# A hybrid mLSTM and delta-rule block on one core: a fourth buffer for weights, more products from rounded halves, gate rows through DRAM, and an earlier split of the delta rule's output

## The chip, the cores and the metric

One core of one Trainium2 chip runs one layer of a bidirectional encoder block. The metric is the device time of one launch in microseconds (us). A profile of one further execution gives the engines' work: PE (TensorE, matrix products), DVE (VectorE), ACT (ScalarE), POOL (GpSimd, here used nearly only to issue DMAs) and SP (SyncE, only issues DMAs).

## The reference, cut to what matters

256 tokens, 2048 channels, all of it in float32:

```python
mod = silu(c) @ ada_w + ada_b                     # six rows of 2048: shift, scale, gate, twice
h = rms_norm(x, norm_mix_w) * (1 + scale_m) + shift_m
proj = h @ w_in                                   # split into a_q a_k a_v a_o, b_qkv, b_z, gates, merge
# branch A: mLSTM, 4 heads, dk 256, dv 512, forwards and backwards
y_a = (sigmoid(a_o) * rms_norm(h_a)) @ w_branch_a
# branch B: gated delta rule, 16 heads, dk = dv = 128, forwards and backwards
qkv = silu(centred_depthwise_conv(b_qkv, gdn_conv_w))
y_b = (rms_norm(o_b) * silu(b_z)) @ w_branch_b
x = x + gate_m * ((g_a * y_a + g_b * y_b) @ w_out)          # gate_m is row 2 of mod
hf = rms_norm(x, norm_ffn_w) * (1 + scale_f) + shift_f
x = x + gate_f * ((silu(gt) * up) @ w_down)                 # gate_f is row 5 of mod
return rms_norm(x, norm_final_w)
```

Both branches are needed in scores: the delta rule needs k·k and q·k of each head, the mLSTM needs q·k and then the sum of the decayed scores times v.

## The kernel before, in words

**Products.** Large products are made from *rounded halves*: of a float32 array `w`, ACT writes `wh`, rounded to the type float32r, and DVE writes `wl = w - wh` (the helper `split`, or the same two instructions inside a job). A product is then `xh·wh + xl·wh + xh·wl`, three passes on PE. A few products still take float32 operands as they are; PE runs such a product as two instructions. Among them are the delta rule's scores `ks` (L571, two of 128x512 a head), the mLSTM's sums over v `ph` (L977, six of 128x512 a head) and the gate rows (`row`, L1088, four of 128x512 for each of two rows).

**Jobs.** Weights stream in as 1 MB tiles `raw` from a pool with three buffers, by DMAs that SP issues in a fixed order. The same three buffers also take the rows of `ada_w` for the sums that make `mod` ("background": `ada_part` loads one 1 MB tile, and one DVE instruction, L126, reduces it). `fjob` multiplies one 128-column block (tiles `raw_b`, `raw_a`), `tjob` one group of 512 columns: four tiles `u`, each in two halves `wh_x_u_0` and `wh_x_u_2`, twelve products of 128x512 for each half. A tile is free for SP when DVE has read it for the last time, and SP's list stands in line: a load whose buffer isn't free holds up all loads behind it.

**Order of the work.** A stage 0 makes `mod`'s first rows, `x` and the first heads (until about 131 us). Then the delta rule runs for four groups of four heads: `gdn_phase1` for each head (convolution, decay, scores `ks`), `gdn_invert` and `gdn_blocks` for a group, and `gdn_phase2` for each pair of heads (a chain of small products `p`, `pa`, `pb`, `pc`, `po`, `px` with ACT and DVE steps between them). Independent jobs (`b`, `a`, `z`, `v`, `o`, `ma`, `mb`) are put between these steps as *fillers*. At the end of a pair the outputs go through DRAM: ACT writes `obt`, stores it (`ob_d`), and POOL loads a group of four heads as `o` (L866). `o_split` makes `obh` and `obl` of it for the projection `yb`. After the delta rule's buffers are given up, `mlstm(h)` for heads 0 and 1, later 2 and 3, is placed between `yb`'s halves. It loads `mkq`, `vt`, `sgo` and twice `bc` on POOL (L917 to L924), makes decays by scans on DVE (`mdec`, L928 to L931), scores `psc` (PE), multiplies both (L946 to L949), and makes `pden` and `ph`. Then come `ya`, `o` with the first residual, gate/up (`gt`, `up`) and down (`d`) of the feed-forward part.

**What sets the order.** The kernel is written as one sequence of instructions; a scheduler of the framework then makes a list for each engine, which runs in that order. Instructions that are wrapped in `order(...)` keep the order in which they are written among themselves, whatever their engine; the rest are placed where the scheduler sees them ready. So an edit in one place can move instructions in others. PSUM is split into four banks for jobs and four for the rest.

Of the kernel before, what the change touches and what calls it, by code (L numbers as in the profile page):

```python
# [52 lines left out]
def hybrid_block(ctx: ExitStack, tc: tile.TileContext, xr, nfr, crow, pk_d, cst_d, ada2, ada4, win0, winb, wint, wba, wbb, wo, wgu, wd, out, dbg=None):  # L53
# [6 lines left out]
    cp = pool(ctx, "cp")  # L60
    st = pool(ctx, "st")
# [35 lines left out]
    c1 = st.tile([1, D], F32, tag="raw", bufs=3, name="c1")  # L97
# [20 lines left out]
    ada_in = [st, "raw", 3]  # L118
# [11 lines left out]


# [16 lines left out]
    def fjob(name, src, done):  # L148

        ps = acc_ps.tile([P, 512], F32, tag="acc", name=f"acc_{name}")  # L150
        o = ps[:, :T]
        raw = st.tile([P, KB, P], F32, tag="raw", bufs=3, name=f"raw_{name}")
        nc.sync.dma_start(raw, src)
        for k0 in range(0, KB, 8):
            wh = st.tile([P, 8, P], F32R, tag="wh", bufs=3, name=f"wh_{name}_{k0}")
            wl = st.tile([P, 8, P], F32R, tag="wl", bufs=3, name=f"wl_{name}_{k0}")
            S.activation(wh, raw[:, k0 : k0 + 8], AF.Copy)  # L157
            V.tensor_tensor(wl, raw[:, k0 : k0 + 8], wh.bitcast(F32), ALU.subtract)  # L158
            for k in range(8):
                for i, x in enumerate((hh, hl)):  # L160
                    PE.matmul(o, wh[:, k], both(x, k0 + k).rearrange("p a b -> p b a"), start=k0 + k + i == 0, stop=False)  # L161
# [7 lines left out]
    def tjob(name, chunks, xh, xl, done, early=0, by_token=None, steps=1):  # L169
# [6 lines left out]
        def halves(u, k0):  # L176
            if u not in raws:
                raws[u] = st.tile([P, 4, 512], F32, tag="raw", bufs=3, name=f"raw_{name}_{u}")
# [3 lines left out]
            order(S.activation(wh, raws[u][:, k0 : k0 + 2], AF.Copy), early)  # L182
            order(V.tensor_tensor(wl, raws[u][:, k0 : k0 + 2], wh.bitcast(F32), ALU.subtract), early)  # L183
            return wh, wl
# [261 lines left out]
    with ExitStack() as s0:  # L446
# [18 lines left out]
        def loads(b):  # L465
            ra = [w0.tile([P, D + 2], F32, tag="ra", bufs=5, name=f"ra{b}_{i}") for i in range(2)]
            raw = st.tile([P, N0, P], F32, tag="raw", bufs=3, name=f"raw0_{b}")
# [73 lines left out]
    def gdn_phase1(h):  # L541
# [13 lines left out]
        sq = fr.tile([P, T], F32, tag="sqq", bufs=1, name=f"sqq{h}")  # L555
# [11 lines left out]
        mi = fr.tile([P, 4, P], F32, tag="mi", bufs=1, name=f"mi{h}")  # L567
        kss = []
        for t in range(2):
            ks = gps(f"ks{h}_{t}")  # L570
            PE.matmul(ks, kq[:, 0, t * P : (t + 1) * P], kq, start=True, stop=True)  # L571
# [343 lines left out]
    def mlstm(h):  # L915
# [19 lines left out]
        for t in range(2):  # L935
# [17 lines left out]
            (0, 0): [(dec[:, 0, 0:P], 0)],  # L953
            (0, 1): [(dec[:, 0, P:256], 0), (dec[:, 0, 256:384], 1)],
            (1, 0): [(dec[:, 1, 256:384], 0), (dec[:, 1, 0:P], 1)],
            (1, 1): [(dec[:, 1, P:256], 1)],
        }
        pd_ = gps(f"pden{h}")
        for (d, t), terms in src.items():
            for i, (w, s) in enumerate(terms):  # L960
                PE.matmul(pd_[:, 2 * t + d : 2 * t + d + 1], w, ones1, start=i == 0, stop=i == len(terms) - 1)
# [8 lines left out]
        yield  # L970
        for t in range(2):
            pn = []
            for d in range(2):
                ph = gps(f"ph{h}_{t}_{d}")
                terms = src[d, t]
                for i, (w, s) in enumerate(terms):
                    PE.matmul(ph, w, vt[:, s], start=i == 0, stop=i == len(terms) - 1)  # L977
# [4 lines left out]
            yield  # L982
# [19 lines left out]
    def y_b(g):  # L1002
# [6 lines left out]
        return tjob(f"yb{g}", [wbb[g, u] for u in range(4)], obh, obl, done)  # L1009
# [30 lines left out]
    for g in range(3):  # L1040
        fill(2)
        o_split(g, o4s[g])
# [10 lines left out]
    mg = mgp.tile([P, 2, D], F32, name="mg")  # L1053

# [8 lines left out]
    for g in range(4):  # L1063
        if g == 3:
            every[0] = 0
        run(y_a(g, mgh, mgl))
    while len(background) > 2:
        sums()
# [11 lines left out]
    def row(part, dst, rp, factor=1.0):  # L1080

        for g in range(4):
            dg = rp.tile([P, 4, P], F32, tag="dg", bufs=2, name=f"dg{part}_{g}")
            for e in range(4):
                c = part * KB + 4 * g + e
                V.tensor_scalar(dg[:, e], ident, mod[:, c : c + 1], factor, ALU.mult, ALU.mult)
            pr = gps(f"row{part}_{g}")
            PE.matmul(pr, ones, dg.rearrange("p e c -> p (e c)"), start=True, stop=True)  # L1088
            S.activation(dst[:, g * 512 : (g + 1) * 512], pr, AF.Copy)

    gm = wp.tile([P, D], F32, name="gm")
    row(2, gm, wp, 0.5)
# [64 lines left out]
    ada_in[:] = [st, "raw", 3]  # L1157
# [84 lines left out]
    row(5, gf, dp)  # L1242
# [134 lines left out]
```

## Time and profile before

| | us |
|---|---|
| median of three runs (1995.4, 1998.9, 2001.5) | 1998.9 |
| the profiled execution, its time | 1998.51 |
| its span from the first to the last instruction | 1996.5 |
| PE busy | 1935.0 (97%) |
| DVE busy | 1392.7 (70%) |
| ACT busy | 1020.6 (51%) |
| POOL busy | 94.7 (5%) |
| DMA: moved in all | 485.64 MB, mean 243 GB/s |

PE's busy time counts from the start of a product to its modelled end, and successive products overlap, so a busy PE still says nothing of how densely it works; the starts of successive products do. An engine's idle time matters here where PE has nothing to do.

### The profile page before, as it was taken

The page shows a single profiled execution, that of the slowest core. Times are in us where ns is not written, and L with a number is a line of the kernel's source. Part 1 is how long each engine was busy: PE and PEld are TensorE (multiplying, and loading weights), DVE is VectorE, ACT ScalarE, POOL GpSimd, SP SyncE. Part 2 cuts the span into 40 slices and gives each one's busy share as a digit, 9 for nine tenths or more (in the row PEclk, how much of TensorE's full clock was granted, in tenths as well). Part 3 has the DMA queues.
Part 4 walks back from the last instruction along what each step waited for, and adds up shares of the span by engine and source line. Part 5 has one row for each costly group of instructions (what it writes and reads, how often), then busy time and mean ns, then how long its engine had stood idle before and what let it go on. Part 6 is the DMA issues. An engine that isn't in the chain of part 4 may idle for free.

```text
span 1996.5 us, 26938 instructions
## 1 busy us (share of the span) xinstructions
PE 1935.0 (97%) x10310; PEld 1697.5 (85%) x10310; DVE 1392.7 (70%) x2099; ACT 1020.6 (51%) x1558; POOL 94.7 (5%) x181
## 2 busy tenths in 40 slices
PE   8998999999999889999899999899999999999997
PEld 6887889988989888989777888688888888888886
DVE  5777987778988787865677779765666665555554
ACT  3145757754774566555453444554444444444443
POOL 0001200110100010100100000000000000000000
PEclk9998999999999999999999999999999999999999
DMA  9986674567676665876787679457676675555553
GB/s 400 420 355 193 197 231 169 177 200 256 209 237 222 212 197 208 284 284 238 298 313 259 241 279 413 166 218 261 235 267 237 232 268 199 208 205 198 209 200 138
DMA packets 78322, 485.64 MB, mean 243 GB/s; under 512 B 10201, under 2 KB 15585, under 8 KB 23793
## 3 DMA queue, kind: packets, MB, share of 16 engines
q1 hardware_dynamic: 63360, 450.95, 62.2%
q0 software_dynamic: 7520, 17.88, 4.3%
q10 hardware_dynamic: 7314, 15.10, 2.0%
q8 instruction: 81, 1.33, 0.3%
q14 instruction: 47, 0.39, 0.1%
HBM read 467.07 MB, written 16.82 MB: 242 GB/s over the span
## 4 chain that ended last, share of the span: by engine, by line
PE 78%; DMA 9%; DVE 7%; ACT 4%; issue 2%; ACTq 0%; POOL 0%; SPq 0%; DVEq 0%; POOLq 0%
PE acc_up L200 4%; PE acc_up L203 4%; PE acc_up L201 4%; PE acc_d L203 4%; PE acc_d L201 4%; PE acc_d L200 4%; PE acc_gt L201 4%; PE acc_gt L200 4%; PE acc_gt L203 4%; DMA ra<-ada 3%; PE acc_b L161 3%; PE acc_o L203 2%; PE acc_o L200 2%; PE acc_o L201 2%; PE acc_a L161 2%; DMA raw_b<-winb 2%
## 5 line engine op out<-in xcount | busy, mean ns | idle before, releaser
L183 DVE TENSOR_TENSOR wl_d<-raw_d,wh_d 128x1024 fp32r<-128x1024 f32 x88 | 107.7, 1224 | 102.3 <-ACT wh_d L182 100.3
L183 DVE TENSOR_TENSOR wl_up<-raw_up,wh_up 128x1024 fp32r<-128x1024 f32 x88 | 107.7, 1225 | 101.2 <-ACT wh_up L182 101.2
L126 DVE SCALAR_TENSOR_TENSOR ada<-ada,crow 128x2048 f32<-128x2048 f32 x64 | 146.4, 2288 | 41.9 <-DMA ada<-ada 41.8
L182 ACT ACTIVATE wh_d<-raw_d 128x1024 fp32r<-128x1024 f32 x88 | 93.0, 1057 | 128.5 <-PE acc_d L201 122.8
L182 ACT ACTIVATE wh_gt<-raw_gt 128x1024 fp32r<-128x1024 f32 x88 | 92.9, 1056 | 120.7 <-PE acc_gt L201 73.2
L182 ACT ACTIVATE wh_up<-raw_up 128x1024 fp32r<-128x1024 f32 x88 | 93.0, 1057 | 120.5 <-PE acc_up L201 72.9
L183 DVE TENSOR_TENSOR wl_gt<-raw_gt,wh_gt 128x1024 fp32r<-128x1024 f32 x88 | 107.1, 1223 | 68.1 <-ACT wh_gt L182 47.3
L161 PE MATMUL acc_b<-hh,wh_b 128*128 128x256 f32 x576 | 140.8, 285 | 7.7 <-ACT wh_b L157 7.7
L161 PE MATMUL acc_b<-hl,wh_b 128*128 128x256 f32 x576 | 141.2, 286 | 0.0
L200 PE MATMUL acc_gt<-wh_gt,hfh 128*128 128x512 f32 x352 | 135.7, 385 | 0.1
L201 PE MATMUL acc_gt<-wh_gt,hfl 128*128 128x512 f32 x352 | 135.0, 384 | 0.0
L200 PE MATMUL acc_up<-wh_up,hfh 128*128 128x512 f32 x352 | 133.4, 379 | 0.0
L201 PE MATMUL acc_up<-wh_up,hfl 128*128 128x512 f32 x352 | 133.4, 379 | 0.0
L200 PE MATMUL acc_d<-wh_d,ffh 128*128 128x512 f32 x344 | 130.8, 380 | 0.0
L201 PE MATMUL acc_d<-wh_d,ffl 128*128 128x512 f32 x344 | 130.8, 380 | 0.0
L515 PE MATMUL first<-x,raw 128*128 128x256 f32 x512 | 114.5, 382 | 7.6 <-ACT x L508 7.6
L161 PEld LDWEIGHTS acc_b<-hh,wh_b 128*128 128x128 f32 x576 | 112.7, 196 | 9.9 <-ACT wh_b L157 8.3
L515 PEld LDWEIGHTS first<-x,raw 128*128 128x128 f32 x512 | 96.0, 190 | 26.1 <-ACT x L508 13.6
L161 PEld LDWEIGHTS acc_b<-hl,wh_b 128*128 128x128 f32 x576 | 112.9, 196 | 2.3 <-issue 2.2
L158 DVE TENSOR_TENSOR wl_b<-raw_b,wh_b 128x1024 fp32r<-128x1024 f32 x72 | 87.4, 1219 | 32.1 <-ACT wh_b L157 31.5
L157 ACT ACTIVATE wh_b<-raw_b 128x1024 fp32r<-128x1024 f32 x72 | 75.1, 1055 | 58.2 <-DMA raw_b<-winb 31.0
L182 ACT ACTIVATE wh_o<-raw_o 128x1024 fp32r<-128x1024 f32 x64 | 67.2, 1056 | 64.7 <-PE acc_o L201 27.2
(370 smaller groups left out, 4990.8 us busy)
## 6 DMA issues: line engine op xcount, KB each, us to landing
ada<-ada SPq DMA_DIRECT2D x64, 1024.0 KB, 5.2
raw_gt<-wgu SPq DMA_DIRECT2D x44, 1024.0 KB, 5.3
raw_up<-wgu SPq DMA_DIRECT2D x44, 1024.0 KB, 5.0
raw_d<-wd SPq DMA_DIRECT2D x44, 1024.0 KB, 4.9
raw_b<-winb SPq DMA_DIRECT2D x36, 1024.0 KB, 5.9
ra<-ada SPq DMA_DIRECT2D x32, 1025.0 KB, 15.7
raw<-win SPq DMA_DIRECT2D x16, 1024.0 KB, 14.5
raw_z<-wint SPq DMA_DIRECT2D x16, 1024.0 KB, 5.6
```

What stands on the lines that cost most here:

```text
L126: V.scalar_tensor_tensor(raw, raw, 1.0, row_c[:, :D], ALU.mult, ALU.mult, accum_out=mod[:, c0 + b : c0 + b + 1])
L157: S.activation(wh, raw[:, k0 : k0 + 8], AF.Copy)
L158: V.tensor_tensor(wl, raw[:, k0 : k0 + 8], wh.bitcast(F32), ALU.subtract)
L161: PE.matmul(o, wh[:, k], both(x, k0 + k).rearrange("p a b -> p b a"), start=k0 + k + i == 0, stop=False)
L182: order(S.activation(wh, raws[u][:, k0 : k0 + 2], AF.Copy), early)
L183: order(V.tensor_tensor(wl, raws[u][:, k0 : k0 + 2], wh.bitcast(F32), ALU.subtract), early)
L200: order(PE.matmul(ps[t], tok(xh, kk, t), turns(wh[:, k]), start=kk == 0, stop=False), early and steps > 1)
L201: PE.matmul(ps[t], tok(xl, kk, t), turns(wh[:, k]), start=False, stop=False)
L203: PE.matmul(ps[t], tok(xh, kk, t), turns(wl[:, k]), start=False, stop=kk == last)
L515: PE.matmul(first[o], raw[:, o], x[:, b], start=b == 0 and o % 2 == 0, stop=b == KB - 1 and o % 2 == 1)
```

## The change

It does the following:

- `raw` has four buffers in place of three, everywhere. To make room, the SBUF set aside for POOL's DMAs is set to 4096 bytes a partition, and `sqq` shares the buffer of `mb`.
- The scores `ks` are made from rounded halves of `kq`: a `split` on ACT and DVE for each head (`kqh`, `kql`, 128x512), then three products in place of one.
- The sums over v `ph` are made from rounded halves of `dec` and `vt` (`dch`, `dcl`, 128x768, and `vth`, `vtl`, 128x1024, once a head), three products in place of one. One `yield` of `mlstm` moves behind its loop, so the fillers between the two halves of `t` go.
- A gate row is no longer multiplied out of the identity: one transpose of 16 columns of `mod`, a copy on ACT, a store to DRAM and a load that repeats the row on all partitions, both DMAs on POOL.
- `o_split` is written ahead of two fillers in place of behind them, and the halves of tile `u = 1` of the first `yb` job are kept in program order (`held`), on ACT and on DVE.

```diff
+    kqp = pool(ctx, "kqp")
-        raw = st.tile([P, KB, P], F32, tag="raw", bufs=3, name=f"raw_{name}")
+        raw = st.tile([P, KB, P], F32, tag="raw", bufs=4, name=f"raw_{name}")
...
+    row_d = {part: tc.dram_tile([D], F32, name=f"row_d{part}") for part in (2, 5)}
+    def row_store(part, rp, factor=1.0):
+        pr = gps(f"row{part}")
+        PE.transpose(pr[0:KB, 0:P], mod[:, part * KB : (part + 1) * KB], ident)
+        sm = rp.tile([KB, P], F32, name=f"rowsm{part}")
+        S.activation(sm, pr[0:KB, 0:P], AF.Copy, scale=factor)
+        G.dma_start(row_d[part].rearrange("(b p) -> b p", b=KB), sm)
+    def row_load(part, dst):
+        G.dma_start(dst, row_d[part].partition_broadcast(P))
...
-            order(S.activation(wh, raws[u][:, k0 : k0 + 2], AF.Copy), early)
-            order(V.tensor_tensor(wl, raws[u][:, k0 : k0 + 2], wh.bitcast(F32), ALU.subtract), early)
+            hold = early or 2 * u + k0 // 2 in held
+            order(S.activation(wh, raws[u][:, k0 : k0 + 2], AF.Copy), hold)
+            order(V.tensor_tensor(wl, raws[u][:, k0 : k0 + 2], wh.bitcast(F32), ALU.subtract), hold)
...
+        kqh, kql = (kqp.tile([P, 2, T], F32R, tag=n, bufs=1, name=f"{n}{h}") for n in ("kqh", "kql"))
+        split(kqh, kql, kq)
-            PE.matmul(ks, kq[:, 0, t * P : (t + 1) * P], kq, start=True, stop=True)
+            c = slice(t * P, (t + 1) * P)
+            PE.matmul(ks, kqh[:, 0, c], kqh, start=True, stop=False)
+            PE.matmul(ks, kqh[:, 0, c], kql, start=False, stop=False)
+            PE.matmul(ks, kql[:, 0, c], kqh, start=False, stop=True)
...
+        split(dch, dcl, dec)
+        split(vth, vtl, vt)
         for t in range(2):
             pn = []
             for d in range(2):
                 ph = gps(f"ph{h}_{t}_{d}")
-                for i, (w, s) in enumerate(terms):
-                    PE.matmul(ph, w, vt[:, s], start=i == 0, stop=i == len(terms) - 1)
+                terms = [(x, y, *q) for x, y in ((dch, vth), (dcl, vth), (dch, vtl)) for q in src[d, t]]
+                for i, (x, y, c, s) in enumerate(terms):
+                    PE.matmul(ph, x[:, d, c : c + P], y[:, s], start=i == 0, stop=i == len(terms) - 1)
...
-        return tjob(f"yb{g}", [wbb[g, u] for u in range(4)], obh, obl, done)
+        return tjob(f"yb{g}", [wbb[g, u] for u in range(4)], obh, obl, done, held=() if g else (2, 3))
...
     for g in range(3):
+        o_split(g, o4s[g])
         fill(2)
-        o_split(g, o4s[g])
...
+            row_store(2, ml, 0.5)
         run(y_a(g, mgh, mgl))
...
-    row(2, gm, wp, 0.5)
+    row_load(2, gm)
...
-    row(5, gf, dp)
+    row_store(5, dp)
+    row_load(5, gf)
...
-    nc = _bacc.Bacc("TRN2", target_bir_lowering=False, num_devices=1)
+    nc = _bacc.Bacc("TRN2", target_bir_lowering=False, num_devices=1, dynamic_dma_scratch_size=4096)
```

The lists of the engines differ in many places. SP's keeps its order up to the first loads of `yb`. Three places matter below. In the names, digits behind `acc_ma` or `po` are the token tile or the pair, and the numbers behind the last underscore are the scheduler's own.

The first is on PE, at the end of the last pair of the delta rule. Before, `px` of the last head stands in the middle of the filler `ma`, with 21 more products of `ma` behind it:

```order
L201 MATMUL acc_ma_0_9042<-wh_ma_3_0_9176,hl 128x512
L200 MATMUL acc_ma_1_9043<-wh_ma_3_0_9176,hh 128x512
L776 MATMUL px_1_8694<-cst,on_8709 128x128 x2
L201 MATMUL acc_ma_1_9043<-wh_ma_3_0_9176,hl 128x512
L200 MATMUL acc_ma_0_9042<-wh_ma_3_0_9176,hh 128x512
```

In the change the fillers are used up after `pa` and eight more products, and `pb`, `pc`, `po` (rows of the same kind left out) and `px` follow each other bare, up to the first product of `yb`:

```order
L218 MATMUL acc_ma_1_9176<-wl_ma_3_2_9326,hh 128x512
L775 MATMUL pb_1_8773<-z_1_8728,gg_7349 128x128 x2
L775 MATMUL pb_1_8773<-z_1_8728,gg_7594 128x128 x2
L763 MATMUL pc_1_8799<-r_1_8729,UL 128x128
L764 MATMUL pc_1_8799<-r_1_8729,UL 128x128
L785 MATMUL po_1_8826<-z_1_8728,at_7350 128x128
...
L790 MATMUL po_1_8826<-z_1_8728,at_7595 128x128
L796 MATMUL px_1_8827<-cst,on_8841 128x128 x2
L796 MATMUL px_1_8827<-cst,on_8842 128x128 x2
L215 MATMUL acc_yb_0_9366<-wh_yb_0_0_9370,obh 128x512
```

What moved: the last pair's chain stands later against its fillers, by 21 products.

The second is on PE as well, where the mLSTM begins. `psc`, `pden` and `ph` of head 0 are those with the lower numbers, those of head 1 the others. Before, they stand one by one between the products of `yb` (this piece is the scores of head 1, with tile 3 of the first `yb` job under way):

```order
L201 MATMUL acc_yb_1_9231<-wh_yb_3_0_9390,obl 128x512
L200 MATMUL acc_yb_0_9230<-wh_yb_3_0_9390,obh 128x512
L937 MATMUL psc_9131<-mkq_8841 128x256 x4
L961 MATMUL pden_9271<-ones,mdec_9112 128x1 x6
L201 MATMUL acc_yb_0_9230<-wh_yb_3_0_9390,obl 128x512
L200 MATMUL acc_yb_1_9231<-wh_yb_3_0_9390,obh 128x512
```

In the change they stand in a block, behind the two halves of tile 0 and ahead of the first product with tile 1:

```order
L218 MATMUL acc_yb_1_9367<-wl_yb_0_2_9387,obh 128x512
L957 MATMUL psc_9250<-mkq_8965 128x256 x4
L957 MATMUL psc_9264<-mkq_8974 128x256 x4
L981 MATMUL pden_9407<-ones,mdec_9245 128x1 x6
L981 MATMUL pden_9422<-ones,mdec_9259 128x1 x2
L1002 MATMUL ph_0_0_9516<-vth_9510,dch_9508 128x512
L1002 MATMUL ph_0_0_9516<-vth_9510,dcl_9509 128x512
...
L1002 MATMUL ph_1_1_9537<-vtl_9511,dch_9508 128x512
L215 MATMUL acc_yb_0_9366<-wh_yb_1_0_9439,obh 128x512
```

What moved: 53 products of `yb` (all of tiles 1 and 2, five of tile 3) stood ahead of the scores of head 1 before; now they stand behind them, and behind the first sums over v.

The third is on DVE at the same time. `wl_yb_u_k` are the lower halves of `yb`'s weights, `obl` those of the delta rule's outputs (`o_0` to `o_3` are the four groups), `mdec` the decays. Before:

```order
L183 TENSOR_TENSOR wl_yb_1_0_9304<-raw_yb_1_9301,wh_yb_1_0_9303 128x1024
L913 TENSOR_TENSOR obl<-o_0_8084,obh 128x1024
L913 TENSOR_TENSOR obl<-o_1_8086,obh 128x1024
L126 SCALAR_TENSOR_TENSOR ada_7_9369,mod<-ada_7_9369,crow 128x2048
L913 TENSOR_TENSOR obl<-o_2_8443,obh 128x1024
L183 TENSOR_TENSOR wl_yb_1_2_9320<-raw_yb_1_9301,wh_yb_1_2_9319 128x1024
L183 TENSOR_TENSOR wl_yb_2_0_9338<-raw_yb_2_9335,wh_yb_2_0_9337 128x1024
L913 TENSOR_TENSOR obl<-o_3_8830,obh 128x1024
```

In the change:

```order
L933 TENSOR_TENSOR obl<-o_2_8576,obh 128x1024
L933 TENSOR_TENSOR obl<-o_3_8963,obh 128x1024
L261 TENSOR_TENSOR vtl_9511<-vt_8967,vth_9510 128x1024
L948 SCALAR_TENSOR_TENSOR mdec_9245<-bc_8971,cst 128x256
...
L1005 SCALAR_TENSOR_TENSOR hs_9419<-ph_0_1_9520,dn_9414,hs_9419 128x512
L985 TENSOR_TENSOR dn_9429<-dn_9429,mT 128x2 x2
L986 RECIPROCAL dn_9429<-dn_9429 128x4
L198 TENSOR_TENSOR wl_yb_1_0_9440<-raw_yb_1_9437,wh_yb_1_0_9439 128x1024
```

What moved: the half `wl_yb_1_0`, and its `wh_yb_1_0` on ACT, stand behind all four `obl`, the decays of both heads and the first `ph`.

More of the change, by code (lines that the diff above doesn't have):

```diff
@@ L96, in hybrid_block @@
     cp.tile([P, 20], F32, name="edge")
-    c1 = st.tile([1, D], F32, tag="raw", bufs=3, name="c1")
+    c1 = st.tile([1, D], F32, tag="raw", bufs=4, name="c1")
     S.dma_start(c1, crow.unsqueeze(0))
@@ L167, in fjob, with tjob @@
             yield True
-    def tjob(name, chunks, xh, xl, done, early=0, by_token=None, steps=1):
+    def tjob(name, chunks, xh, xl, done, early=0, by_token=None, steps=1, held=()):
         raws = {}
@@ L177, in halves @@
             if u not in raws:
[L178 removed]
+                raws[u] = st.tile([P, 4, 512], F32, tag="raw", bufs=4, name=f"raw_{name}_{u}")
                 nc.sync.dma_start(raws[u], chunks[u])
@@ L553, in gdn_phase1 @@
         )
-        sq = fr.tile([P, T], F32, tag="sqq", bufs=1, name=f"sqq{h}")
+        sq = fr.tile([P, T], F32, tag="mb", bufs=1, name=f"sqq{h}")
         S.activation(sq, kq[:, 1], AF.Square)
@@ L970, in mlstm @@
         yield
+        dch, dcl = (mp.tile([P, 2, 384], F32R, name=f"d{n}{h}", tag=f"d{n}", bufs=1) for n in ("ch", "cl"))
+        vth = ml.tile([P, 2, DV_A], F32R, tag="o4", bufs=1, name=f"vth{h}")
+        vtl = mp.tile([P, 2, DV_A], F32R, tag="vtl", bufs=1, name=f"vtl{h}")
+        split(dch, dcl, dec)
+        split(vth, vtl, vt)
         for t in range(2):
@@ L1053, in hybrid_block @@
     mg = mgp.tile([P, 2, D], F32, name="mg")
+    mp = pool(sd, "mp", side="right")
     every[0] = 2
@@ L1078, in hybrid_block @@
     S.dma_start(x1, xr)
[L1080 to L1089, printed above, removed]
     gm = wp.tile([P, D], F32, name="gm")
-    row(2, gm, wp, 0.5)
+    row_load(2, gm)
     def residual(t, g, ps, gate, ss, rp, hold=False):
```

25 lines of the change are left out of this document (12 added, 13 removed).

## The prediction, made before the changed kernel ran

> **What bounds the kernel now.** I read the head of the page first, then the busy time by stretches, then what PE waits for, and last the chain of work that ended last.
>
> ```profile
> span 1996.5 us, 26938 instructions
> PE 1935.0 (97%) x10310; PEld 1697.5 (85%) x10310; DVE 1392.7 (70%) x2099; ACT 1020.6 (51%) x1558; POOL 94.7 (5%) x181
> PE 78%; DMA 9%; DVE 7%; ACT 4%; issue 2%; ACTq 0%; POOL 0%; SPq 0%; DVEq 0%; POOLq 0%
> ```
>
> PE is busy for 97% and carries 78% of the chain: what PE no longer does is gained nearly in full, and what makes PE wait is lost. DVE and ACT matter only where PE waits for them. The profiled execution took 1998.51, 2.0 more than its span, and lies 0.4 under the median of the three runs. The windows show two places where PE isn't fed (columns: length, PE busy, PEld, DVE, ACT, POOL, granted clock, DMA share, GB/s):
>
> ```profile
> 0.00:123.00 123.00, 112.85 (x490) 91.92 (x490) 83.43 (x97) 24.20 (x47) 2.41 (x12) 1.00 1.00 412
> 160.00:960.00 800.00, 777.26 (x4985) 707.79 (x4984) 624.81 (x1238) 496.88 (x908) 79.93 (x148) 0.99 0.67 220
> 640.00:760.00 120.00, 109.09 (x796) 102.06 (x795) 93.28 (x174) 72.50 (x148) 9.09 (x17) 0.97 0.62 210
> 662.20:665.60 3.40, 3.40 (x18) 3.40 (x18) 3.33 (x6) 2.71 (x5) 0.00 (x0) 0.50 0.33 48
> 744.10:747.50 3.40, 3.40 (x18) 3.40 (x17) 3.40 (x5) 3.06 (x7) 0.00 (x0) 0.50 0.03 10
> 972.80:979.60 6.80, 4.46 (x10) 3.10 (x11) 4.52 (x5) 3.79 (x6) 3.65 (x7) 0.50 1.01 379
> ```
>
> In 640 to 760 PE is idle for 10.9 us, about half of the 22.7 between 160 and 960, and twice the granted clock falls to 0.50 for 3.4 us, which costs 1.7 each. The third half-clock stretch is the passage from the delta rule to the mLSTM. The waits name the causes:
>
> ```profile
> PE acc_b L161 <- ACT wh_b L157: 7.7, 4, 2.7
> PE acc_yb L200 <- DMA ada<-ada: 6.0, 1, 6.0
> ```
>
> **The change part by part.**
>
> *Fewer passes.* Successive products of rounded operands, and the float32 ones:
>
> ```profile
> 1500.40 0.38 PE L200 MATMUL acc_gt<-wh_gt,hfh 128*128 128x512 f32 x1
> 1500.62 0.38 PE L201 MATMUL acc_gt<-wh_gt,hfl 128*128 128x512 f32 x1
> ```
>
> ```profile
> 341.27 1.72 PE ks L571 x4
> ```
>
> ```profile
> L571 PE MATMUL ks<-kq 128*128 128x512 f32 x64 | 31.2, 597 | 0.0
> L977 PE MATMUL ph<-vt,mdec 128*128 128x512 f32 x48 | 22.0, 594 | 0.0
> L1088 PE MATMUL row<-dg,ones 128*128 128x512 f32 x16 | 8.2, 592 | 0.0
> ```
>
> A rounded product takes 0.216 from start to start. A float32 product is two instructions, and the chain gives two of them (x4) 1.72, so 0.86 each. Three passes are 0.65: 0.21 saved a product. `ks` has 64/2 = 32 products, 6.8; `ph` 24, 5.1; the gate rows' 8 products go whole, 6.9, against two small transposes, 0.4 as an estimate. Together **−18.4**; all of it is PE time and PE is the bound, so its own bounds are narrow, −17 to −20.
>
> *The fourth tile.* The four waits of `acc_b` (7.7 us in all) lie in 640 to 760; the chain shows the first, and the wait of SP's list behind it:
>
> ```profile
> 646.01 4.89 DMA ada<-ada
> ...
> 653.25 7.12 DMA raw_b<-winb
> ```
>
> ```profile
> SPq L153 <- DVE ada L126: 63.7, 11, 10.9
> ```
>
> The load of `raw_b` goes out only at 653.25, when DVE's sum over an `ada` tile has freed the buffer; 7.1 later it lands, and PE is out of work. SP's order is unchanged there, so with a fourth buffer the load goes out one freeing earlier, and with 210 GB/s moved in this window against 412 at the start the DMA engines have room. Gain: 7.7 of waits and two half-clock stretches, 3.4: **−11**. Bounds: 0 (the sum on DVE is what is late, and a later slot waits instead) to all 10.9 idle and 3.4, −14.3. I take the waits named, since the row says which load was late. The row above of 662.2 to 665.6 shows half clock behind a wait of at most 2.7. The Trainium skill ("TensorE: Matmul & The Clock Gate", Part 1, on the clock gate's two states) lets the clock drop after an idle window of about 3.4 us; by that these stretches would not hang on such waits, and the saving would be 7.7, the sum 3.4 higher; the trace speaks against it.
>
> *The splits.* Their nearest rows are those of weights, twice the size of `kqh` and `kql` (128x512), of the size of `vth` and `vtl`:
>
> ```profile
> L158 DVE TENSOR_TENSOR wl_b<-raw_b,wh_b 128x1024 fp32r<-128x1024 f32 x72 | 87.4, 1219 | 32.1 <-ACT wh_b L157 31.5
> L157 ACT ACTIVATE wh_b<-raw_b 128x1024 fp32r<-128x1024 f32 x72 | 75.1, 1055 | 58.2 <-DMA raw_b<-winb 31.0
> ```
>
> 16 heads by 0.53 on ACT and 0.61 on DVE are 8.4 and 9.8. In 160 to 960, ACT is idle for 303 and DVE for 175 us, and the fillers cover: 0. If the cover fails in each head, PE waits 1.14 sixteen times, 18. I take **+2**, nearer to nothing, for the fillers stand between the steps of a head nearly everywhere.
>
> *Gate rows, the smaller scratch, `sqq`.* A row of 1 MB comes through POOL's queue; its 0.5 MB loads take 7.9 (`o`, below), so 16 as an estimate. The row of `gm` is used 96 products of `o` later (20.7 us), that of `gf` 264 products of `d` later (57 us): hidden, **0**; if not, the end of a 16-us load, 1 to 5. `sqq` in `mb`'s buffer is written before `mb` in the same head: 0. POOL with a smaller scratch may have to wait for its own DMAs before it issues more: 0, and at most another landing like the 7.9 of `o`, which the upper bound of the passage takes in.
>
> *The passage to the mLSTM.* `o_split` stands ahead of the fillers, and the last pair uses them up: `pb`, `pc`, `po`, `px` follow each other bare. How long PE stands then is read from ACT's and DVE's steps between `pc` and `po`, and between `po` and `px`:
>
> ```profile
> 944.25 0.37 ACT L747 ACTIVATE z<-pc,sm 128x128 f32<-128x128 f32 x1 [2.85 <-PE pc L744]
> ...
> 945.02 0.38 ACT L748 ACTIVATE z<-pc,sm 128x128 f32<-128x128 f32 x1
> ...
> 951.17 0.28 ACT L789 ACTIVATE on<-po 128x128 f32<-128x128 f32 x1 [2.91 <-PE po L770]
> ...
> 953.33 1.28 ACT L793 ACT_TABLE_LOAD   x1
> 954.62 0.21 ACT L793 ACTIVATE so<-so 128x4 f32<-128x4 f32 x1
> ...
> 964.57 0.48 ACT L778 ACTIVATE obt<-px,pk 128x256 f32<-128x256 f32 x1 [0.67 <-PE px L776]
> 965.08 0.33 ACTq L779 DMA_DIRECT2D ob_d<-obt  x1
> ```
>
> ```profile
> 955.08 1.13 DVE L799 SCALAR_TENSOR_TENSOR on<-po,so,sz 128x128 f32<-128x128 f32 x4
> ```
>
> `pc` to `po`: 1.2. `po` to `px`: 951.17 to 956.21 less a half of `ma` of 1.06 in between, 4.0. `pb` to `pc` about 0.9 (estimate, one such step fewer). Sum 6.1 idle. Then comes the load of the last outputs, and behind it on POOL's queue those of the mLSTM:
>
> ```profile
> ob_d<-obt ACTq DMA_DIRECT2D x16, 128.0 KB, 4.3
> o<-ob_d POOLq DMA_DIRECT2D x4, 512.0 KB, 7.9
> mkq<-kq_d POOLq DMA_DIRECT2D x4, 512.0 KB, 12.1
> ```
>
> ```profile
> 971.47 0.81 POOL L866 DMA_DIRECT2D o<-ob_d  x1 [123.51 <-ACT wh_yb L182]
> ```
>
> ```profile
> 999.80 0.69 DVE L930 TENSOR_TENSOR_SCAN mdec<-bc,cst 128x256 f32<-128x256 f32 x1
> ```
>
> ```profile
> 988.15 1.73 PE psc L937 x8
> ...
> 997.86 1.23 PE pden L961 x12
> ```
>
> Counted from the end of the last `px`: two `obt` with their stores 1.6, the store's landing 4.3, so `o` goes out at 5.9. Before, 77 products of `yb` were there to cover what follows. Now PE has tile 0 (24 products, 5.2), and then, ahead of tile 1, `psc` of both heads (3.5), `pden` (1.2) and `ph` of head 0 (18, 3.9): 13.8. Behind `o` some 4 MB of POOL's and 3 MB of SP's loads are under way; at the 412 GB/s of the kernel's start this is 17 us (the row of 972.8 shows 379), so the last `bc` lands at 22.9; scans, scores and their products, 2.7; `pden` and `ph`, 4.9: tile 1 starts at 30.5, and PE has stood for 16.7. With 6.1 and 3.4 of half clock (two stretches) 26. Before, the same place cost 6.0 of wait, 2.2 of half clock (4.46 busy at 0.50) and, as an estimate, 0.8 of smaller gaps: 9. Net **+17**. Bounds: the decays of head 1 came 28.3 behind `o` before (971.47 to 999.80), which makes it +30; if they land 9 sooner than I say, +8.
>
> The sum: 1996.5 − 18.4 − 11 + 2 + 17 = 1986 of span, with 2.0 around it **1988**.
>
> **The rivals.** *The passage is cheap.* With fewer loads of SP's beside them, POOL's land some 10 us earlier: PE stands 6.7 in place of 16.7 and the second half clock goes, −13: 1975. For it: before, `yb`'s and `ada`'s loads shared the DMA engines. Against it: 12.1 for a 0.5-MB load. The Trainium skill ("DMA: Bandwidth & Descriptors", the part on one DMA issued by GpSimd) gives about 2.0 us and then 436 GB/s, by which 0.5 MB takes an estimated 3.2 and the time would be nearer to this rival; the rows of 7.9 and 12.1 disagree.
>
> *The fourth tile saves nothing.* If DVE's sum is late in itself, the buffer that comes free earlier is filled with the next tile in SP's line, and `acc_b` waits as before: 1988 + 11 = 1999, no change. For it: the 63.7 us of SP's wait stand behind DVE 11 times. Against it: the load, 7.1, and the wait for `ada`'s DMA lie on the chain, not DVE's queue.
>
> *The last group's chain lacks fillers* (the one on the other side). `o_split` and the fillers' new place leave less work on PE between the first `p` of group 3 and its last `px`.
>
> ```profile
> 858.79 0.97 PE L697 MATMUL p<-R,cc 128*128 128x32 f32 x8
> ```
>
> ```profile
> 917.82 0.86 PE L697 MATMUL p<-R,cc 128*128 128x32 f32 x7
> ```
>
> ```profile
> 964.15 0.38 PE L776 MATMUL px<-cst,on 128*128 128x128 f32 x2
> ```
>
> Before, this took 105 us (858.79 to 964.3) with PE full; in the change the products that PE's list has there add up to 77 (at the starts above), and 83 with the 6.1 of above. If the chain of ACT, DVE and DMA steps needs the whole 105, PE stands for 22 more: 2010. It is slower from a need of 100 us on (83 + 17). For it: nothing in the trace shows the chain alone. Against it: PE waited inside it nowhere for long, and the second pair took 46 us (917.82 to 964.15) with fillers between all its steps.
>
> **How the numbers follow.** 0.3%, 6 us, is about what a measurement here can tell from no change: faster is under 1992.9, slower over 2004.9. My forecast 0.45, with its own range 1976 to 1996: some 0.36 faster, 0.09 the same. Cheap passage 0.25, all faster. Fourth tile without effect 0.16: 0.03 faster, 0.11 the same, 0.02 slower. Lack of fillers 0.14: 0.02 the same, 0.12 slower. So faster 0.64, the same 0.22, slower 0.14. The range: low end with all of the fourth tile, 14.3, and the passage free, 1998.5 − 18.4 − 14.3 = 1966; the high end 2004 takes in the fourth tile without effect and the passage 5 worse, and leaves out most of the last rival.
>
> **What the changed kernel's profile would show.** `ks` 96 and `ph` 72 products, no `dg`; PE's busy time some 18 less. No wait of `acc_b` for `wh_b` near 660 to 745, and no half clock there; else the second rival. In the delta rule no new waits of `ks` for `kqh` or `kql` over 2 us in all. At the passage, waits of `px` for `on` (4), of the first `yb` for `obh`, of `psc` or `pden` for `bc` or `mdec`, about 10 to 20 in all, and the granted clock at 0.50 behind them; under 10 is the first rival. A long wait of PE for `p`, `pa` or `pc` between 830 and 950 is the third. I am wrong altogether if a lack of work appears elsewhere in the delta rule, where the lists moved as well, or if `gm` and `gf` come late to the residuals.

## The result and the profile after

| | before | changed |
|---|---|---|
| median of 7 runs (lowest to highest), us | 1996.6 (1990.2 to 2001.5) | 1983.5 (1976.6 to 1986.4) |
| the profiled execution, us | 1998.51 | 1979.27 |
| its span, us | 1996.5 | 1977.3 |

The ratio is 0.9936, 95% interval 0.9921 to 0.995: 13 us faster by the medians. The two profiled executions lie 19.2 apart, since the one of before is a long one of its kind and the one of the change a short one. A second set of runs of the same changed kernel gave 0.9934 (0.9915 to 0.9954) and a profiled span of 1981.0. So 1988 was 4.5 us too long, in its range, and its side and size were right. The steps under it were right only in part.

The head of the page after:

```profile
span 1977.3 us, 27036 instructions
PE 1918.9 (97%) x10352; PEld 1705.5 (86%) x10352; DVE 1402.5 (71%) x2091; ACT 1022.7 (52%) x1568; POOL 96.9 (5%) x185
PE 73%; DVE 11%; DMA 9%; ACT 4%; issue 2%; POOL 0%; SPq 0%; ACTq 0%; DVEq 0%; POOLq 0%
```

PE is as full as before, at 97%, of a shorter span, but only 73% of the chain are PE's now and DVE has 11%: the waits have another place. The same three stretches of both kernels, in the order before, after: the delta rule, the passage with the mLSTM, the entry of the feed-forward part (columns as in the prediction's windows):

```profile
160.00:930.00 770.00, 747.26 (x4769) 679.31 (x4768) 610.98 (x1219) 481.13 (x876) 79.93 (x148) 0.99 0.68 222
930.00:1100.00 170.00, 163.80 (x809) 135.95 (x809) 115.84 (x158) 80.83 (x119) 12.37 (x21) 0.98 0.76 278
1200.00:1320.00 120.00, 110.71 (x500) 93.05 (x499) 93.61 (x111) 63.40 (x95) 0.00 (x0) 0.97 0.69 267
```

```profile
160.00:930.00 770.00, 762.62 (x4993) 705.77 (x4992) 634.75 (x1248) 494.42 (x899) 80.03 (x148) 1.00 0.69 231
930.00:1100.00 170.00, 155.10 (x720) 132.89 (x719) 118.89 (x169) 83.05 (x127) 12.37 (x21) 0.92 0.69 251
1200.00:1320.00 120.00, 108.35 (x498) 92.89 (x497) 92.43 (x109) 61.33 (x89) 0.00 (x0) 0.96 0.67 261
```

In the delta rule PE idles 7.4 us where it idled 22.7, and the clock stays at full speed. At the passage it idles 14.9 in place of 6.2 and the mean clock falls from 0.98 to 0.92. Of PE's waits in the change (in all, times, longest), those at the passage and at the entry of the feed-forward part:

```profile
PE pxn L1200 <- ACT xn L1193: 11.6, 7, 6.8
...
PE psc L957 <- DMA mkq<-kq_d: 3.7, 2, 3.3
PE acc_yb L215 <- ACT obh L932: 3.5, 1, 3.5
PE px L796 <- DVE on L819: 3.5, 2, 3.3
...
PE pb L775 <- DVE r L776: 2.3, 1, 2.3
```

The waits of `acc_b` for `wh_b` (7.7) and the one of 6.0 before `yb` are gone. In their place stand the bare pair (`pb`, `px`), the first `yb` behind `obh`, and `psc` behind `mkq`. Two long stretches at half clock lie there:

```profile
946.00:956.20 10.20, 5.81 (x14) 3.67 (x15) 4.46 (x7) 3.90 (x5) 4.82 (x8) 0.50 0.47 157
966.50:980.20 13.70, 13.21 (x44) 11.38 (x43) 7.28 (x19) 6.29 (x10) 2.00 (x4) 0.50 0.47 156
```

They cost about 9.5, half of the busy time in them (5.81 and 13.21). The sum of the two profiles can be closed with a count over PE's starts: each product's start less the one before it, above what such a product takes undisturbed. What it gives in all depends on what is taken as undisturbed; the differences hardly do. With 0.216 for a rounded product of 128x512 and 0.43 for an instruction of a float32 one, PE lost as much before as after. The delta rule (100 to 900) lost 22 less, the passage and the mLSTM (900 to 1100) some 19 to 20 more, the entry of the feed-forward part (1200 to 1400) 1 more; the rest is small. So the 19 us between the profiles are the work that PE no longer does, 18.5 by the lists and these prices. By the starts measured further down the work is nearer to 16, and 3 us of the 19 are fewer losses.

### The profile page after: what moved, and what is told of

Read it like the earlier page. It is cut to its first block, busy times and chain, and to the rows that moved or that the text cites. A ratio compares the mean times of both kernels' runs of the same rounds, so it can differ in the third digit from the quotient of the medians.

```text
span 1977.3 us, 27036 instructions
## 1 busy us (share of the span) xinstructions
PE 1918.9 (97%) x10352; PEld 1705.5 (86%) x10352; DVE 1402.5 (71%) x2091; ACT 1022.7 (52%) x1568; POOL 96.9 (5%) x185
## 4 chain that ended last, share of the span: by engine, by line
PE 73%; DVE 11%; DMA 9%; ACT 4%; issue 2%; POOL 0%; SPq 0%; ACTq 0%; DVEq 0%; POOLq 0%
DMA ra<-ada 5%; PE acc_up L215 4%; PE acc_up L218 4%; PE acc_up L216 4%; PE acc_d L216 4%; PE acc_d L215 4%; PE acc_d L218 4%; PE acc_gt L216 4%; PE acc_gt L215 4%; PE acc_gt L218 4%; PE acc_o L218 2%; PE acc_o L216 2%; PE acc_o L215 2%; PE acc_a L175 2%; PE acc_b L175 2%
## 5 line engine op out<-in xcount | busy, mean ns | idle before, releaser
L175 PE MATMUL acc_b<-hh,wh_b 128*128 128x256 f32 x576 | 134.6, 276 | 0.0
L175 PE MATMUL acc_b<-hl,wh_b 128*128 128x256 f32 x576 | 134.6, 277 | 0.0
L218 PE MATMUL acc_gt<-wl_gt,hfh 128*128 128x512 f32 x352 | 95.3, 385 | 0.0
## 6 DMA issues: line engine op xcount, KB each, us to landing
raw<-win SPq DMA_DIRECT2D x16, 1024.0 KB, 17.1
```

The lines of the kernel that those rows point to most:

```text
L218: PE.matmul(ps[t], tok(xh, kk, t), turns(wl[:, k]), start=False, stop=kk == last)
```

## The experiments

Below, "idle" is a window's length less PE's busy time, the two windows are 160 to 930 and 930 to 1100, and "clock" is the granted clock in the second. The ratios are to the kernel before.

| run | ratio, interval | idle, delta rule | idle, passage | clock |
|---|---|---|---|---|
| before | 1 | 22.7 | 6.2 | 0.98 |
| changed | 0.9936, 0.9921 to 0.995 | 7.4 | 14.9 | 0.92 |
| after_again | 0.9934, 0.9915 to 0.9954 | 8.0 | 16.6 | 0.92 |
| held_undone | 0.9921, 0.9902 to 0.994 | 7.7 | 15.2 | 0.93 |
| three_tiles | 1.0082, 1.006 to 1.0103 | 23.1 | 19.4 | 0.91 |
| ks_float32 | 1.0006, 0.9989 to 1.0023 | 10.0 | 19.7 | 0.88 |
| tiles_alone | 1.001, 0.9991 to 1.003 | 13.4 | 15.9 | 0.94 |
| rows_by_product | 0.996, 0.9943 to 0.9976 | 9.0 | 21.2 | 0.94 |
| fillers_kept | 1.006, 1.0038 to 1.0082 | 32.0 | 13.6 | 0.93 |
| kept_not_held | 0.9998, 0.9981 to 1.0014 | 33.1 | 8.7 | 0.97 |
| old_mlstm | 0.9961, 0.9945 to 0.9978 | 9.7 | 17.1 | 0.94 |
| no_tile_no_ks | 1.0039, 1.0018 to 1.0061 | 20.5 | 11.6 | 0.94 |
| sums_float32 | 0.9994, 0.9974 to 1.0015 | 8.5 | 19.0 | 0.93 |
| fillers_spread | 0.9962, 0.9947 to 0.9977 | 20.3 | 13.3 | 0.96 |

The table gives one profile each, and runs of one kernel spread over 4 to 21 us, so idle times a few us apart say little. Idle time also leaves out what the half clock costs; where the text speaks of the count over the starts, that cost is in it.

**The change once more.**

> The changed kernel once more, beside the runs below on the same chip. Its ratio to the kernel before should again be 0.992 to 0.995. If its profiled execution lies some 5 us from the first one's 1979.3, its waits should show which stretches differ from one execution to the next: I expect the delta rule (loads that land sooner or later), not the feed-forward part.

The ratio came out as expected. The profiled span was 3.7 longer. Against the expectation the delta rule hardly differed (8.0 idle, 7.4 before). The passage had 1.7 more idle, and the half-clock stretch at the entry of the feed-forward part was 10.2 long in place of 6.8.

**Fourth buffer alone, and all but the fourth buffer.** First the kernel before with four buffers:

```diff
-        raw = st.tile([P, KB, P], F32, tag="raw", bufs=3, name=f"raw_{name}")
+        raw = st.tile([P, KB, P], F32, tag="raw", bufs=4, name=f"raw_{name}")
... (so at every raw; sqq in mb's buffer, scratch 4096)
```

> The kernel before with only the fourth buffer for raw (and what makes room for it, the smaller scratch and the shared buffer of sqq). Its list has the last pair of the delta rule bare as in the change, but the mLSTM's scores between the products of yb. Theory A (the fourth buffer takes some 20 us of waits out of the delta rule and costs some 10 at the passage): 8 to 12 us faster than before, ratio 0.994 to 0.996. Theory B (what it gains in the delta rule it gives back at the passage): within 3 us of before.

Theory B held: the delta rule idles 9.3 less (13.4 for 22.7), the passage 9.7 more at a lower clock, and the time is the same. By the count over the starts the delta rule loses some 14 less than before and the passage some 17 more. Its waits at the passage are those of the change, though neither `o_split` nor `yb`'s halves were touched:

```profile
PE px L776 <- DVE on L799: 6.8, 2, 3.5
...
PE acc_yb L200 <- ACT obh L912: 3.5, 1, 3.5
PE pb L755 <- DVE r L756: 3.5, 1, 3.5
...
PE psc L937 <- DMA mkq<-kq_d: 2.9, 1, 2.9
```

So the fourth buffer alone is enough to make the last pair bare. The engines' lists say how: fillers are a fixed stock, and what fills a wait early is missing late. Counted with undisturbed starts, PE's list has some 25 us more work up to the last `px` of the third group than before with four buffers alone, and some 20 more in the change, whose `ks` take less; the fillers in it are drawn from the same jobs.

Then the change with three:

```diff
-        raw = st.tile([P, KB, P], F32, tag="raw", bufs=4, name=f"raw_{name}")
+        raw = st.tile([P, KB, P], F32, tag="raw", bufs=3, name=f"raw_{name}")
... (so at every raw)
```

> The changed kernel with three buffers for raw in place of four, all else as in the change. Theory A (the fourth buffer gives 15 us in 640 to 800 and some 4 each at 187 and 486, and takes the fillers from the last pair, so that PE waits there for 8 us and runs at half clock): the waits of acc_b for wh_b come back, pb, pc, po and px have fillers between them again; 8 to 14 us slower than the changed kernel, ratio to before 0.998 to 1.001. Theory B (the fourth buffer gives back at the passage all that it gains in the delta rule): within 3 us of the changed kernel.

Neither theory: 30 us slower than the change (2012.2 and 1982.4 in these runs), over twice what A said. The delta rule is back at 23.1 idle, as A had it, but the passage got worse, not better (19.4, clock 0.91). The last pair did not get its old list back: `pb` and `pc` have fillers between them again, but between `po` and `px` only three products of `ma` are left, and PE waits there:

```profile
PE px L796 <- DVE on L819: 6.7, 1, 6.7
...
PE acc_yb L215 <- ACT obh L932: 5.5, 1, 5.5
```

So the rest of the change draws fillers away from the pair as well. The fourth buffer is worth nothing to the kernel before and some 30 us to the rest of this change.

**The held halves of `yb`.**

```diff
-        return tjob(f"yb{g}", [wbb[g, u] for u in range(4)], obh, obl, done, held=() if g else (2, 3))
+        return tjob(f"yb{g}", [wbb[g, u] for u in range(4)], obh, obl, done, held=())
```

> The changed kernel without the held halves of yb: psc of head 0 stands behind 32 products of yb and psc of head 1 behind 48, not behind 24 both. Theory A (the held halves put the mLSTM's scores ahead of tile 1, and PE waits there for POOL's loads, 4.7 us and a half-clock stretch of 13.7 us behind it, 6.9 lost): 8 to 12 us faster than the changed kernel, ratio to before 0.987 to 0.989, no wait of psc for mkq. Theory B (PE only waits elsewhere, for the next yb tile or for the decays): within 2 us of the changed kernel, 0.993 to 0.994.

2.5 us faster by the medians, with intervals that overlap; nearer to B. The wait of `psc` for `mkq` fell to 0.9, as A said. But PE waited 1.8 for a half of `yb` at 1049 with 10.2 of half clock behind, and the passage kept its 15 us of idle.

**The scores from float32.**

```diff
-        split(kqh, kql, kq)
...
-            PE.matmul(ks, kqh[:, 0, c], kqh, start=True, stop=False)
-            PE.matmul(ks, kqh[:, 0, c], kql, start=False, stop=False)
-            PE.matmul(ks, kql[:, 0, c], kqh, start=False, stop=True)
+            PE.matmul(ks, kq[:, 0, t * P : (t + 1) * P], kq, start=True, stop=True)
```

> The changed kernel with the delta rule's scores from float32 kq again, without the two split instructions a head. Theory A (PE is the bound and the splits are covered): 5 to 8 us slower than the changed kernel (6.8 of PE work, and a few us either way at the passage, where eight more fillers are left), ratio to before 0.996 to 0.998. Theory B (the splits on ACT and DVE cost as much as the passes save): within 2 us of the changed kernel.

A by its sign, at twice the size: 14 to 16 us slower. Some 5 to 7 of it is PE's work. The delta rule has 2.6 more idle without the splits, so no cost of the splits shows there. Most of the rest is the passage (19.7 idle, clock 0.88).

**The gate rows by products.**

```diff
-    row_load(2, gm)
+    row(2, gm, wp, 0.5)
... (row() as before; so for part 5)
```

> The changed kernel with the gate rows by products out of the identity again. The sums over ada no longer stand between the steps of the last residual on DVE. Theory A (the rows through DRAM save 6.5 us of PE work and cost 3.5 of wait of pxn for xn and 1.7 of half clock at the entry of the feed-forward part): 1 to 3 us slower than the changed kernel, ratio to before 0.994 to 0.995, and the wait of pxn back at 3.5 longest. Theory B (the rows' place has nothing to do with that wait): 6 to 7 us slower, 0.9965 to 0.997.

Between the two: 0.996, about 5 us slower than the change. The wait that A named did go back:

```profile
PE pxn L1210 <- ACT xn L1203: 8.4, 7, 3.4
```

In the change this wait is 6.8, and DVE's timeline there shows what stands in it: a sum over `ada` between two steps of the last residual, and a second one behind them, ahead of what PE waits for.

```profile
1251.16 0.69 DVE L1113 TENSOR_TENSOR tmss<-acc_o,gm 128x512 f32<-128x512 f32 x1 [1.14 <-PE acc_o L241]
1251.77 2.28 DVE L127 SCALAR_TENSOR_TENSOR ada<-ada,crow 128x2048 f32<-128x2048 f32 x1
1253.98 0.08 DVE L127 DVE_READ_ACCUMULATOR ada<-ada,crow 128x1 f32 x1
1253.98 0.69 DVE L1114 TENSOR_TENSOR x<-x,tmss 128x512 f32<-128x512 f32 x1
```

It is 3.4 also in `tiles_alone` and in `three_tiles`, so it takes the fourth buffer and the new rows together.

**The mLSTM's part.** The sums from float32 with the rest kept, then the whole of the mLSTM's part as before, then that part and the rows without the fourth buffer and without the scores:

```diff
-                terms = [(x, y, *q) for x, y in ((dch, vth), (dcl, vth), (dch, vtl)) for q in src[d, t]]
+                terms = [(x, y, *q) for x, y in ((dec, vt),) for q in src[d, t]]
...
-        yield
+            yield
```

> The changed kernel with the sums over v from float32 again and the yield back inside the loop, the held halves and the early split of the outputs kept. Theory A (PE work is gained one for one): 3 to 6 us slower than the changed kernel, ratio 0.995 to 0.9965. Theory B (the splits that the sums need at the passage cost as much): within 2 us of it.

A by its sign, larger: some 12 us slower than the change by the ratios. Some 4 to 5 of it is PE's work; in the profile, which is one of its shorter executions, the rest is idle at the passage (19.0).

```diff
... (as above, and)
-        return tjob(f"yb{g}", [wbb[g, u] for u in range(4)], obh, obl, done, held=() if g else (2, 3))
+        return tjob(f"yb{g}", [wbb[g, u] for u in range(4)], obh, obl, done, held=())
...
-        o_split(g, o4s[g])
         fill(2)
+        o_split(g, o4s[g])
```

> The changed kernel with the mLSTM and its surroundings as before: sums over v from float32, the yield inside the loop, no held halves, the outputs split behind the fillers. What is left of the change is the fourth buffer, the scores from halves and the gate rows. Theory A (the sums from halves are worth their 5.1 us of PE work, the block of held halves costs 2 or 3): 1 to 5 us slower than the changed kernel, ratio to before 0.994 to 0.996. Theory B (the mLSTM's part costs more at the passage than it saves): 3 or more us faster than the changed kernel, under 0.992.

A, at the end of its range: 0.9961, 5 us slower than the change. So the mLSTM's part as a whole is worth about its PE work, and with float32 sums the held halves and the early `o_split` together cost about 7 (0.9994 and 0.9961).

```diff
... (three_tiles and ks_float32 together)
```

> The changed kernel with three buffers and the scores ks from float32: what is left is the mLSTM's part and the gate rows, with 11.6 us less of PE work than before, and the last pair with its fillers as before. Theory A (where the last pair isn't bare, the block of held halves costs some 10 us, as the two runs with kept fillers differ): 4 us faster to 2 slower than before, ratio 0.998 to 1.001. Theory B (the block costs 2 or 3, as its undoing in the change showed): 7 to 10 us faster, 0.995 to 0.9965.

Slower than both theories, 1.0039, though it has 11.6 us less work for PE than before (by the lists) and its last pair has all its fillers. The delta rule idles about as before, the passage 5.4 more at 0.94; by the count over the starts it loses 12 more than before. The bare pair has no part in that: here the block of scores ahead of `yb`'s tile 1 is what PE waits in (7.8 for `mkq`), at about the size of A.

**The fillers kept for the last group.** In the chains of the last four heads products of every step, and some of each filler between them, are pinned behind the instruction written before them, and more of the fillers are written ahead of the group and between its steps:

```diff
-        fill(8)
+        fill(8 if g < 3 else 12)
...
+                tail[0] = int(g == 3)
...
-                PE.matmul(pb[:, e, i], hd[e][1][:, i], z[:, e, 3 * i], start=True, stop=True)
+                order(PE.matmul(pb[:, e, i], hd[e][1][:, i], z[:, e, 3 * i], start=True, stop=True), tail[0])
```

> The changed kernel with the fillers of the last group of heads pinned in the order in which they are written, so that every step of both pairs has 2.6 to 7.7 us of them behind it, as before; held halves of yb as in the change. Theory A (the bare pair costs 7.7 of waits, 3.9 before the first yb, and the half clock behind them): the waits of pb, po and px go, the block of scores keeps its 4 to 5 us; 10 to 15 us faster than the changed kernel, ratio to before 0.986 to 0.989. Theory B (the steps before, inverse and blocks of the last group, need the fillers that now come later): PE waits there as long, and the time is within 3 us of the changed kernel.

Neither: 25 us slower than the change. The last pair is no longer bare, but its group's inverse has 41 us of work beside it in place of 73 (by the lists), and PE waits there in one piece:

```profile
PE p L718 <- DVE R L690: 17.5, 2, 17.2
...
PE psc L961 <- DMA mkq<-kq_d: 8.6, 2, 4.8
PE pb L776 <- DVE r L777: 7.7, 2, 6.1
```

This is B's mechanism, and more than B's price: 20.5 us of half clock lie in and behind the wait (13.7 of them while PE stands), and 20.5 more from 984 on. The same without the held halves (`held=()`):

> As the run with kept fillers, and without the held halves of yb, so that scores and sums of the mLSTM stand between yb's products. Theory A (the block costs PE its waits for mkq and for the decays): 3 to 6 us faster than with the held halves. Theory B (without the held halves PE waits for the second pair's yb halves instead, as the run without them showed): within 2 us of it.

A by its sign, at over twice the size: 13 us faster than with the held halves (1994.2 and 2007.5), by idle (8.7 for 13.6) and clock (0.97 for 0.93) at the passage. The wait of `psc` for `mkq` falls from 8.6 to 0.4. Where fillers are left for the pair, the held halves are what PE waits at.

Last, the fillers spread in another way, without the held halves:

```diff
-        fill(8 if g < 3 else 12)
+        fill(8 if g < 3 else 19)
... (fewer pieces between the steps of the two pairs)
```

> A version meant to beat both: the changed kernel without the held halves, and with the fillers of the last group pinned so that the inverse keeps 59 us of them (41 in the run that kept too many, 73 in the change) and each step of the pairs 2.6 to 7.7. Theory A (the waits are then short everywhere and no long half-clock stretch follows): no wait over 3 us between 760 and 1000, some 8 us less lost to half clock; 8 to 15 us faster than the changed kernel, ratio 0.986 to 0.989. Theory B (the fillers are a fixed stock, and what is given to one step is missing in another, waits and half clock alike): within 3 us of the run without the held halves, 0.990 to 0.994.

B in kind, and slower than its range: the long waits of the chain went, but the first `yb` now waits 10.8 for `obh`, and with 0.9962 the kernel is some 5 us slower than the change, at intervals that just overlap. Of all runs, that without the held halves is the best, 0.9921, not told apart from the change (0.9936). No version that clearly beats both came out.

## Why the prediction was right, and where it was not

**Fewer passes, −18.4: right in kind, some 2 too large.** The list has 96 `ks`, 72 `ph` and two transposes, each form a third of the passes:

```profile
L589 PE MATMUL ks<-kqh 128*128 128x512 f32 x32 | 14.0, 437 | 0.2 <-DVE at L623 0.2
L1002 PE MATMUL ph<-vth,dcl 128*128 128x512 f32 x24 | 9.2, 441 | 0.0
L138 PE MATMUL row<-cst,mod 128*16 128x128 f32 x2 | 0.5, 272 | 0.0
```

PE's busy time fell by 16.1, and the span of the profiled pair by 19.2. The price of a pass was taken from `gt`, where successive products start 0.216 apart. Those of `ks` start further apart:

```profile
225.88 0.40 PE L589 MATMUL ks<-kqh 128*128 128x512 f32 x1
226.11 0.40 PE L590 MATMUL ks<-kql,kqh 128*128 128x512 f32 x1
226.35 0.40 PE L591 MATMUL ks<-kqh,kql 128*128 128x512 f32 x1
226.58 0.38 PE L215 MATMUL acc_v<-wh_v,hh 128*128 128x512 f32 x1
```

Three take 0.70, not 0.65, and the median of all `ks` and `ph` is the same to 0.01. So a product saves 0.16 and not 0.21, and the term is about −16. The undoings cost more than the work alone (14 to 16 where I had 6.8, about 12 where I had 5.1); what is above it lies at the passage, where each undoing also draws other lists.

**The fourth tile, −11: mis-sized, and its other half was booked elsewhere.** The waits of `acc_b` and the half clock behind them went as said. In the window of the prediction:

```profile
640.00:760.00 120.00, 118.31 (x892) 112.67 (x891) 104.50 (x200) 85.60 (x166) 9.09 (x17) 1.00 0.72 246
```

Idle fell from 10.9 to 1.7 there, and from 22.7 to 7.4 over the whole delta rule, with its 17 us of half-clock stretches gone: some 22 in the count over the starts (some 14 with the fourth buffer alone), more than my term and outside its bounds, which took only 640 to 760. But the step that failed is another: I took these waits for pure gain. `tiles_alone` shows that the same fillers are then missing at the last pair: net 0.

**The splits, +2:** with four buffers nothing of it shows; the delta rule with float32 scores idles 10.0, with halves 7.4. What they do move is the list: with three buffers the kernel with them is slower than without (1.0082 and 1.0039), and by the count over the starts that lies at the passage.

**The gate rows, 0: too good.** The rows come in time (`gm` lands 10 us, `gf` 39 us ahead of its first use), but the sums that moved with them stand in the residual: about 3.4 of wait at `pxn`, and by the run with products about 5 of the 6.5 are left.

**The passage, +17: the size right, the cause and the parts wrong.** It lost 19 more by the count over the starts. I blamed `o_split`'s place for the bare pair. But `old_mlstm`, with `o_split` behind the fillers again, has the same order of products there, from `pa` to `px`, and `tiles_alone` has the bare pair without it.

The pair's waits were near (7.7 for 6.1, by the starts: 2.4, 0.9, 3.5, 0.9). The wait for the loads was half of mine: 3.5 for `obh`, 3.7 for `psc` and about 1 for `pden` and `ph`, 8 to 9 for 16.7. `o` went out 3.2 behind the last `px` (948.23 to 951.38), where I had 5.9. The half clock took 9.5 where I had 3.4. So tile 1 started 32.4 behind the last `px` (980.67), near my 30.5 with its 3.4 of half clock, but PE stood half as long as I said and worked at half speed instead. These two errors met, and that the term came out near is in part luck.

The held halves, on which the term for the loads hung, cost 2.5 in the change, 7 with float32 sums (there with the early `o_split`) and 13 with kept fillers; it looks as if that wait and the bare pair cover each other.

One more correction, to the text on the kernel: in its third list the held half stands behind `hs` and `dn` too, which are not in `order`. So `order` seems to pin an instruction behind whatever was written before it on its engine, and the held halves stand behind the mLSTM's first steps; this is read from the lists alone.

**The sum.** For the two profiles it is 19.2 where I had 10.5. With the passes at my price, the delta rule gave 22 where I had 9 (−11 and +2), the passage took 19 to 20 where I had 17, and some 2 more went elsewhere. That the medians lie only 13 apart, near my figure, is in part luck too.

**The rivals.** The cheap passage didn't come as a whole. Its wait did: PE stood 8 to 9 for the loads, nearer to its 6.7 than to my 16.7, but the half clock, which it had shrink, grew. That the fourth tile saves nothing is true of it alone, by another way than I gave: the wait passes to the end of the delta rule, not to the next slot. The lack of fillers in the last group, my case on the slower side, is the real mechanism of the passage; in the change it cost 8 for the pair, and `fillers_kept` shows its full form, 17.2 at the inverse.

What stays open: why the fourth buffer is worth 30 us with the rest of the change and nothing without. The count over the starts says where. Of the 31 between the profiles of the change and of `three_tiles`, 24 lie in the delta rule and 6 at the passage; alone, the fourth buffer gains some 14 in the delta rule and gives them back at the passage. And with float32 scores it is worth only some 7 (`no_tile_no_ks` 1.0039, `ks_float32` 1.0006), so most of the 30 comes with the scores from halves. But the passage differs with each list (idle 8.7 to 21.2, clock 0.88 to 0.97), and no run here separates the order of the lists from the half clock that goes with it.

## What to carry to other kernels

When independent work covers a chain of latencies, it is a stock: count how much of it is left at the chain's end before booking a removed wait as a gain. Work that the bound engine no longer does is the part of such a change that can be relied on, here some 16 of 19; take its price from products of the same kind. Look in the lists for where a wait comes back, and price a wait with the slow clock that follows it.

## What the hardware showed

But for the one that ends with the program, the half-clock stretches are 3.4, 6.8, 10.2, 13.7, 17.1 or 20.5 us long, and one can follow a wait of PE far shorter than the first of them. In `no_tile_no_ks`, PE's timeline and a window:

```profile
315.14 0.94 PE L711 MATMUL p<-R,cc 128*128 128x32 f32 x7 [1.23 <-issue]
```

```profile
316.80:320.20 3.40, 3.40 (x19) 3.40 (x18) 2.31 (x5) 2.57 (x5) 0.00 (x0) 0.50 0.07 14
```

1.23 of wait and a row of narrow products, then 3.4 at 0.50 while PE had work throughout. The Trainium skill ("TensorE: Matmul & The Clock Gate", Part 1) describes a window of about 3.4 us that runs freely; the lengths here agree with that. It also asks for a whole idle window before the clock falls, which this row doesn't show.

In the change the clock even fell with no wait of PE at all, behind the `pden` of two heads in a row (24 products of 128x1):

```profile
1052.17 2.73 PE L981 MATMUL pden<-ones,mdec 128*128 128x1 f32 x24
```

```profile
1051.80:1055.20 3.40, 3.40 (x29) 3.32 (x28) 3.40 (x4) 1.11 (x3) 0.00 (x0) 1.00 0.93 318
1055.20:1058.60 3.40, 3.40 (x10) 2.69 (x9) 0.85 (x7) 0.47 (x1) 0.00 (x0) 0.50 1.02 422
```

Eight other runs show such a drop at the second two heads of the mLSTM, with 18 to 24 `pden` in the 3.4 us before it and PE busy for at least 3.37 of them. So half clock can follow a block of narrow products where no wait shows; here it cost about half of 3.4. Nor did a busy PE end a stretch at once: in the change PE was busy for 13.21 of the 13.70 us from 966.5 on, with `psc`, `pden` and `ph`, at half clock throughout.
